# One first transfer for weight half, tokens and gains; latent attention twelve steps later in a two-layer trunk on one core

## The chip, the core and the metric

The kernel runs on one core of a Trainium2 chip. The metric is the device time of one execution in microseconds (us). The runs of the kernel before took 802.56, 802.88 and 804.34 us, with a median of 802.88 us. The execution that was profiled took 802.21 us; its span, from the first instruction to the last, is 800.4 us.

## The reference

Two layers run over 256 tokens of 1024 numbers, in fp32. The part that matters here:

```python
for l in range(DEPTH):
    h = rmsnorm(x, g_pre_mix[l])
    (c_q, c_kv, k_r, p_in, s_u, s_v, cv_b, cv_c, cv_x,
     gate_logits) = split_cols(h @ w_in[l])
    y_a = mla_branch(c_q, c_kv, k_r, ...) @ w_br_a[l]     # latent attention
    y_b = pool_branch(p_in, ...) @ w_br_b[l]
    y_c = sgu_branch(s_u, s_v, ...) @ w_br_c[l]
    y_d = conv_branch(cv_b, cv_c, cv_x, ...) @ w_br_d[l]
    gates = sigmoid(gate_logits).reshape(B, S, N_BRANCH, D)
    merged = sum over the four branches of gate * y
    x = x + rmsnorm(merged @ w_out[l], g_post_mix[l])
    h = rmsnorm(x, g_pre_ffn[l])
    f = (silu(h @ w_ffn_gate[l]) * (h @ w_ffn_up[l])) @ w_ffn_down[l]
    x = x + rmsnorm(f, g_post_ffn[l])
```

In `mla_branch` the normed `c_q` goes through `w_uq`, the normed `c_kv` through `w_ukv`, and eight heads of a chunk-causal softmax follow.

## The kernel before

**Precision by halves.** Every product is made of three matmuls (`mac`, L318 to L320). A number a is held as a high half (a rounded to TensorE's fast fp32 format, by ScalarE) and a low half (a minus its high half, by VectorE); the kernel adds high times high, low times high and high times low. So each weight that arrives must be split twice, the high half on ScalarE (L268) and then the low half on VectorE (L288), before its last use.

**Pieces.** The weights are cut on the host into pieces of at most 128 x 1024 floats, in the order of use, which `piece_plan` writes out. A piece is fetched by SyncE (SP) into one of four staging buffers `st` (`stage`, L253), split into two of 24 buffers `u`, and used. SP waits at a fetch until the staging buffer's former piece has been split. "A" are the 416 columns of the projection that feed the attention (query latent, key-value latent, rotary key), "S" the 512 of the gating unit, "P" and "C" 512 each for the pooling, the convolution and the rest; each has four pieces, of two 128-row blocks k each. "gd", "gb", "gc" and "ga" are the gates' pieces of the branches in the order d, b, c, a; "y" are the branch projections; "uq" (two) and "ukv" are the attention's own weights.

**Steps.** The kernel has no scheduler: instructions stand on each engine in the order in which the program writes them. The matmuls are written unit by unit, a unit being two blocks of one piece for one half h of the tokens (six matmuls of 512 columns), and after each unit `tick` is called, which is one step. A step also advances the background generators, among them `g_att` (latent attention) and `g_misc` (the three other branches), whose `yield n` says how many steps to let pass, and it splits another piece while fewer than five or six untouched ones are ready (`LOW`, `HIGH`). `AS` is the number of steps after which the attention starts, counted from its spawn at step 16 of layer 0, and `PA` the steps between the scaling of its latents and their transposes. In layer 0 the attention starts at step 23, its first projection (uq) runs at step 35, its last product of probabilities and values (L743) at step 81, and the first unit that needs it, the branch projection of a, comes at step 108. Layer 1 has the same distances.

**The start.** Until the first weights are there, TensorE multiplies a tile of zeros `NW` = 7 times (L387). The first inputs come on two queues. ScalarE's queue fetches block 0 of the transposed tokens (`xT`) and then the table `const` (158 columns: rotary tables, pooling counts and, from column 96, the gains). SP's queue fetches, each as a transfer of its own, the first halves of pieces A0 and S0, block 1 of the tokens, the second halves, blocks 2 and 3, the whole pieces A1 and S1, and blocks 4 to 7. The tokens are scaled by the gain while they are split (`x_hi`: block 0 on VectorE, L561, the others on ScalarE, L563; `x_lo` on VectorE, L567), and the halves of A0 and S0 are split at L581 and L582. TensorE's first real matmuls are the 24 of L909, twelve for block 0 (six of 416 columns, six of 512) and twelve for block 1; then the units of A1, S1, A2 and so on follow.

Of the kernel before, what the change touches and what calls it, by code (L numbers as in the profile page):

```python
# [10 lines left out]
F32 = mybir.dt.float32  # L11
F32R = mybir.dt.float32r
# [5 lines left out]
P = 128  # L18
# [18 lines left out]
NTOK = 9  # L37
LOW = 4
GF = 5
GY, MY, AY, AS, MS = 4, 4, 4, 8, 3  # L40
Y1, Y2, Y3, Y4, Y5 = 2, 4, 3, 3, 3
PA, PB = 2, 4
SA, SB = 3, 3
NW = 7
EV = 2
XAT, XD = (8, 9), 8
RN = 1
# [23 lines left out]
SGW = _o  # L71


def down_after(b):

    return [b - DLAG] if 0 <= b - DLAG < NB - DLAST else []


def piece_plan():

    plan = []
    for l in range(NL):
# [111 lines left out]


@with_exitstack
def trunk(ctx: ExitStack, tc, x, xT, wall, small, const, qtab, gpost, out):
    nc = tc.nc
    PS = bass.MemoryType.PSUM
    cp = ctx.enter_context(tc.tile_pool(name="cp", bufs=1))  # L200
# [156 lines left out]


    ident = T([P, P], "ident", 1, pool=cp)
    cst = T([P, 96 + NL * SGW], "cst", 1, pool=cp)  # L360
    warm = T([P, 1], "warm", 1, pool=cp)
    ht = [hT_tiles(h) for h in range(2)]
    state["free"] -= 2
# [6 lines left out]
    nc.scalar.dma_start(cst, const)  # L370
# [12 lines left out]
    nc.vector.memset(warm, 0.0)  # L383
# [170 lines left out]
    sg = gains(0)  # L554
    hT, rstd = [None, None], [None, None]

    def x_hi(k, eng=nc.scalar):
        for h in range(2):
            o, i, g = ht[h][0][:, k, :], xt[k // 4][:, k % 4, h * P:(h + 1) * P], sg["gpm"][:, k:k + 1]
            if eng is nc.vector:  # L560
                nc.vector.tensor_scalar(o, i, g, None, op0=ALU.mult)  # L561
            else:
                nc.scalar.activation(o, i, AF.Identity, scale=g)  # L563

    def x_lo(k):
        for h in range(2):
            nc.vector.scalar_tensor_tensor(ht[h][1][:, k, :], xt[k // 4][:, k % 4, h * P:(h + 1) * P],  # L567
                                           sg["gpm"][:, k:k + 1], ht[h][0][:, k, :].bitcast(F32),
                                           op0=ALU.mult, op1=ALU.subtract)


    first_w = {i: (U([P, PIECE], F32R), U([P, PIECE], F32R)) for i in range(2)}
    state["free"] -= 4
    src = [staged.pop(i) for i in range(2)]
    for k in range(2):
        x_hi(k, nc.vector if k == 0 else nc.scalar)
        x_lo(k)
        for i in range(2):
            w = PLAN[i][1] // 2
            c = np.s_[:, k * w:k * w + w]  # L580
            nc.scalar.activation(first_w[i][0][c], src[i][c], AF.Copy)  # L581
            nc.vector.tensor_tensor(first_w[i][1][c], src[i][c], first_w[i][0].bitcast(F32)[c], op=ALU.subtract)  # L582
    for i in range(2):
        known(i, *first_w[i])
    state["cv"] = 2
# [608 lines left out]
def build(arrays):  # L1194
# [3 lines left out]
    ap = {k: nc.dram_tensor(k, v.shape, F32, kind="ExternalInput").ap() for k, v in arrays.items()}  # L1198
    out = nc.dram_tensor("out", (SEQ, D), F32, kind="ExternalOutput").ap()
    with tile.TileContext(nc) as tc:  # L1200
        trunk(tc, ap["x"], ap["xT"], ap["wall"], ap["small"], ap["const"], ap["qtab"], ap["gpost"], out)
    return nc


def host_arrays(inputs):
    inp = {k: np.asarray(v) for k, v in inputs.items()}
    wall = np.zeros((len(PLAN), P, PIECE), np.float32)
    for i, (key, w) in enumerate(PLAN):
        wall[i, :, :w] = host_piece(inp, key)
    x = np.ascontiguousarray(inp["x"][0])  # L1210
    const, qtab = host_const(inp)
    return {
        "x": x,
        "xT": np.ascontiguousarray(x.T.reshape(NK, P, SEQ).transpose(1, 0, 2)),
        "wall": wall,
        "small": np.stack([host_small(inp, l) for l in range(NL)]),
        "const": const,
        "qtab": qtab,
        "gpost": np.ascontiguousarray(np.stack([inp["g_post_mix"], inp["g_post_ffn"]], axis=1)),
    }  # L1220
# [9 lines left out]
```

## Time and profile before

| what | value |
|---|---|
| median of 3 runs | 802.88 us |
| profiled execution | 802.21 us |
| its span | 800.4 us |
| TensorE busy | 790.8 us (99%) |
| VectorE busy | 598.3 us (75%) |
| ScalarE busy | 452.6 us (57%) |
| moved by DMA | 148.11 MB, mean 185 GB/s |
| from the span's start to the first matmul of L909 | 5.67 us |

A row of the timeline gives the start and the length in us, the engine (PE is TensorE, PEld its weight load, DVE VectorE, ACT ScalarE, a q behind it the engine's queue of instructions), the line, the operation, the tiles written and read, the shape, the count, and in brackets how long the engine had been idle and what ended that. In the DMA view a row gives the tile and its source, the queue, the count, the size and the time from the issue to the landing.

### The profile page before, as it was taken

To read this page: it belongs to the slowest core of one execution; us is meant where nothing else is said; L and a number is where in the kernel's file an instruction comes from. 1 tells how busy PE (TensorE), PEld (TensorE's weight loads), DVE (VectorE), ACT (ScalarE), POOL (GpSimd) and SP (SyncE) were. 2 spreads that over 40 slices of the span, in tenths; PEclk is the share of its full clock that TensorE was granted. 3 is DMA by queue.
4 is the path that set the end of the run, shared out by engine and by line. 5 is a ranking of instruction groups with operands and counts; after the bars stand their busy time and mean duration, and the time that the engine had idled before them with its cause. 6 is when DMAs were issued, how large, how long until landed. Compare 5 with 4: busy or idle time off the path is not lost.

```text
span 800.4 us, 10903 instructions
## 1 busy us (share of the span) xinstructions
PE 790.8 (99%) x3982; PEld 666.3 (83%) x3982; DVE 598.3 (75%) x1094; ACT 452.6 (57%) x776; POOL 3.9 (0%) x16
## 2 busy tenths in 40 slices
PE   8999999999999999999999999999999999999996
PEld 8888887888888888888888888878888888888885
DVE  6687976758887777778895688764679787777773
ACT  7767655444665555455665675644367555455541
POOL 0000000000000000000000000000000000000000
PEclk9999999999999999999999999999999999999999
DMA  9866444465664565555655545455555555555631
GB/s 317 304 215 212 160 158 158 160 208 164 201 214 136 185 205 185 186 192 176 223 170 197 205 161 182 131 172 197 175 193 184 181 185 186 187 185 185 206 106 52
DMA packets 42245, 148.11 MB, mean 185 GB/s; under 512 B 4688, under 2 KB 5840, under 8 KB 42192
## 3 DMA queue, kind: packets, MB, share of 16 engines
q1 hardware_dynamic: 41328, 145.12, 54.4%
q0 software_dynamic: 576, 2.10, 0.8%
q8 instruction: 31, 0.51, 0.3%
q10 hardware_dynamic: 288, 0.21, 0.1%
q14 instruction: 22, 0.18, 0.1%
HBM read 146.36 MB, written 1.05 MB: 184 GB/s over the span
## 4 chain that ended last, share of the span: by engine, by line
PE 98%; DVE 1%; DMA 0%; ACT 0%; issue 0%; DVEq 0%; SPq 0%; ACTq 0%
PE acc L318 20%; PE acc L320 20%; PE acc L319 20%; PE mm L1097 17%; PE mm L1102 9%; PE tp L440 3%; PE mm L318 2%; PE mm L320 2%; PE mm L319 2%; PE mm L715 1%; PE acc L743 1%; PE acc L909 1%; DMA st<-wall 0%; PE mm L836 0%; PE mm L862 0%; DVE mrg L500 0%
## 5 line engine op out<-in xcount | busy, mean ns | idle before, releaser
L288 DVE TENSOR_TENSOR u<-st,u 128x1024 fp32r<-128x1024 f32 (+1 forms) x268 | 318.6, 1214 | 50.6 <-ACT u L268 50.0
L268 ACT ACTIVATE u<-st 128x1024 fp32r<-128x1024 f32 (+1 forms) x268 | 273.5, 1047 | 17.0 <-DMA st<-wall 16.8
L318 PE MATMUL acc<-u,hh 128*128 128x512 f32 (+1 forms) x424 | 169.1, 399 | 0.0
L320 PE MATMUL acc<-u,hh 128*128 128x512 f32 (+1 forms) x424 | 164.5, 388 | 0.0
L319 PE MATMUL acc<-u,hl 128*128 128x512 f32 (+1 forms) x424 | 164.2, 387 | 0.0
L1097 PE MATMUL mm<-u,u 128*128 128x512 f32 x576 | 144.4, 392 | 0.0
L1097 PEld LDWEIGHTS mm<-u,u 128*128 128x128 f32 x576 | 105.3, 188 | 20.8
L318 PE MATMUL acc<-u,s2k 128*128 128x512 f32 x256 | 101.2, 395 | 0.0
L320 PE MATMUL acc<-u,s2k 128*128 128x512 f32 x256 | 100.6, 393 | 0.0
L319 PE MATMUL acc<-u,s2k 128*128 128x512 f32 x256 | 100.3, 392 | 0.0
L320 PEld LDWEIGHTS acc<-u,hh 128*128 128x128 f32 x424 | 79.6, 188 | 16.2
L318 PEld LDWEIGHTS acc<-u,hh 128*128 128x128 f32 x424 | 79.7, 188 | 14.5 <-issue 0.3
L319 PEld LDWEIGHTS acc<-u,hl 128*128 128x128 f32 x424 | 79.8, 188 | 14.2
L1102 PEld LDWEIGHTS mm<-u,u 128*128 128x128 f32 x576 | 78.6, 190 | 5.6
L1102 PE MATMUL mm<-u,u 128*128 128x256 f32 x576 | 80.3, 282 | 0.0
L1025 ACT ACTIVATE gate<-acc,rhalf 128x512 f32<-128x512 f32 x32 | 22.0, 689 | 65.9 <-PE acc L320 65.7
L320 PEld LDWEIGHTS acc<-u,s2k 128*128 128x128 f32 x256 | 48.1, 188 | 10.1
L318 PEld LDWEIGHTS acc<-u,s2k 128*128 128x128 f32 x256 | 48.2, 188 | 9.3 <-issue 0.3
L319 PEld LDWEIGHTS acc<-u,s2k 128*128 128x128 f32 x256 | 48.1, 188 | 9.1
L1108 DVE TENSOR_TENSOR tok<-mm,tok 128x256 f32<-128x256 f32 x72 | 30.3, 420 | 27.7 <-ACT tok L1107 27.5
L1107 ACT COPY tok<-mm 128x256 f32<-128x256 f32 x72 | 26.6, 370 | 42.6 <-PE mm L1102 39.6
L443 ACT ACTIVATE s2k<-tok 128x256 fp32r<-128x256 f32 (+1 forms) x38 | 16.3, 429 | 53.8 <-DVE tok L1122 53.8
(172 smaller groups left out, 750.1 us busy)
## 6 DMA issues: line engine op xcount, KB each, us to landing
st<-wall SPq DMA_DIRECT2D x261, 512.0 KB, 3.8
st<-wall SPq DMA_DIRECT2D x7, 416.0 KB, 4.0
gpost<-gpost POOLq DMA_DIRECT2D x4, 512.0 KB, 4.7
x<-x SPq DMA_DIRECT2D x2, 512.0 KB, 6.0
small<-small SPq DMA_DIRECT2D x2, 512.0 KB, 4.2
u<-xT SPq DMA_DIRECT2D x3, 256.0 KB, 6.2
st<-wall SPq DMA_DIRECT2D x2, 256.0 KB, 4.3
out<-x SPq DMA_DIRECT2D x2, 256.0 KB, 2.0
```

The lines of the kernel that those rows point to most:

```text
L268: nc.scalar.activation(hi[:, :w], st[:, :w], AF.Copy)
L288: nc.vector.tensor_tensor(lo[:, :w], st[:, :w], hi.bitcast(F32)[:, :w], op=ALU.subtract)
L318: nc.tensor.matmul(out_, a[0][aw], w[0][ws], start=start, stop=False)
L319: nc.tensor.matmul(out_, a[1][aw], w[0][ws], start=False, stop=False)
L320: nc.tensor.matmul(out_, a[0][aw], w[1][ws], start=False, stop=stop)
L440: nc.tensor.transpose(dst[:, i * P:(i + 1) * P], s, ident)
L443: nc.scalar.activation(hi, src, AF.Copy)
L1025: nc.scalar.activation(gt[h], pgt[h], AF.Tanh, scale=rhalf[h])
L1097: nc.tensor.matmul(o, pc_[0][:, k * P:(k + 1) * P], hx[k // 2][:, k % 2].rearrange("p s t -> p (s t)"), start=(k == 0), stop=False)
L1102: nc.tensor.matmul(o[:, :SEQ], pc_[1][:, k * P:(k + 1) * P], hx[k // 2][:, k % 2, 0, :], start=False, stop=(k == NK - 1))
L1107: nc.scalar.copy(dst, o[:, SEQ:2 * SEQ])
L1108: nc.vector.tensor_tensor(dst, o[:, 0:SEQ], dst, op=ALU.add)
```

## The change

1. A new input `head` holds, side by side, the first half of A0, block 0 of the tokens and eight columns of gains (680 columns); and in a second part the second half of A0, block 1 of the tokens and the whole table (830 columns). Each part is one transfer on SP's queue into a staging buffer, from which the tokens, the weights and the gains are read directly. ScalarE's queue fetches nothing any more. The table is copied to its own tile `cst` by ScalarE, after the second parts of A0 and S0 have been split.
2. Piece A1 is fetched and split in halves too, between the tokens' blocks 2 and 3. S1, blocks 4 and 5, A2, and blocks 6 and 7 are fetched later in SP's order, behind the copy of the table in the program; S1 has to wait for the staging buffer of the first part.
3. The zeros are multiplied eight times (`NW`).
4. `AS` goes from 8 to 20 and `PA` from 2 to 5: the attention starts at step 35, uq at step 50, the last product of probabilities and values stands at step 96. Its three weight pieces move in the plan behind the eight gate pieces of branch d.

The diff, cut to its core:

```diff
-GY, MY, AY, AS, MS = 4, 4, 4, 8, 3
+GY, MY, AY, AS, MS = 4, 4, 4, 20, 3
-PA, PB = 2, 4
+PA, PB = 5, 4
-NW = 7
+NW = 8
+HA = 416
+HC = HA + SEQ
+HG = SG["gpm"][1]
+CW = 96 + NL * SGW
...
-        plan += [((l, "uq", i), 1024) for i in range(2)]
-        plan += [((l, "ukv", 0), 1024)]
...
+                if br == "b" and n == 0:
+                    plan += [((l, "uq", i), 1024) for i in range(2)]
+                    plan += [((l, "ukv", 0), 1024)]
...
-    xt_load(nc.scalar, 0, 1)
-    nc.scalar.dma_start(cst, const)
-    stage_part(0, 0)
+    heads = [T([P, PIECE], "st", NST, pool=wp)]
+    nc.sync.dma_start(heads[0][:, 0:HC + HG], head[0, :, 0:HC + HG])
     stage_part(1, 0)
-    xt_load(nc.sync, 1, 2)
-    stage_part(0, 1)
+    heads.append(T([P, PIECE], "st", NST, pool=wp))
+    nc.sync.dma_start(heads[1][:, 0:HC + CW], head[1, :, 0:HC + CW])
     stage_part(1, 1)
-    state["dma"] = 2
     xt_load(nc.sync, 2, 4)
-    stage_to(4)
-    xt_load(nc.sync, 4, 6)
-    xt_load(nc.sync, 6, 8)
+    stage_part(2, 0)
+    stage_part(2, 1)
+    state["dma"] = 3
...
+    nc.scalar.copy(cst, heads[1][:, HC:HC + CW])
+    stage_to(4)
+    xt_load(nc.sync, 4, 6)
+    for k in range(2):
+        x_hi(2 + k)
+        x_lo(2 + k)
+        split_part(2, k, src[2][:, HA * k:HA * k + HA])
...
     stage_to(5)
-    for kp in range(1, 4):
+    xt_load(nc.sync, 6, 8)
+    pump(1)
+    settle()
+    for kp in range(2, 4):
```

ScalarE's instructions from the program's start: `u` are split weights, `hh` split tokens, `st` staging buffers, `warm` a dummy. Before:

```order
L367 DMA u_8_76<-xT 128x256
L370 DMA cst_70<-const 128x158
L388 ACT_TABLE_LOAD
L388 ACTIVATE warm_71<-warm_71 128x1
L581 ACTIVATE u_18_112<-st_80 128x416
L581 ACTIVATE u_20_114<-st_82 128x512
L563 ACTIVATE hh_4_72<-u_8_76,cst_70 128x128
L563 ACTIVATE hh_6_74<-u_8_76,cst_70 128x128
L581 ACTIVATE u_18_112<-st_80 128x416
L581 ACTIVATE u_20_114<-st_82 128x512
```

And after, to the same place and on to the first half of A1, which stands between the tokens' blocks:

```order
L394 ACT_TABLE_LOAD
L394 ACTIVATE warm_71<-warm_71 128x1
L590 ACTIVATE u_19_109<-st_78 128x416
L590 ACTIVATE u_21_111<-st_80 128x512
L579 ACTIVATE hh_4_72<-st_82 128x128
L579 ACTIVATE hh_6_74<-st_82 128x128
L590 ACTIVATE u_19_109<-st_82 128x416
L590 ACTIVATE u_21_111<-st_80 128x512
L602 COPY cst_70<-st_82 128x158
L579 ACTIVATE hh_4_72<-u_8_76,cst_70 128x128
L579 ACTIVATE hh_6_74<-u_8_76,cst_70 128x128
L590 ACTIVATE u_23_113<-st_86 128x416
```

The two DMAs are gone from ScalarE, block 1 of the tokens is read from the second head transfer (`st_82`), and the copy of the table has come in ahead of block 2.

SP's queue at the same place, before and after:

```order
L261 DMA st_80<-wall 128x416
L261 DMA st_82<-wall 128x512
L367 DMA u_8_76<-xT 128x256
L261 DMA st_80<-wall 128x416
L261 DMA st_82<-wall 128x512
L367 DMA u_8_76<-xT 128x512
L253 DMA st_88<-wall 128x832
L253 DMA st_90<-wall 128x1024
L367 DMA u_9_77<-xT 128x512 x2
```

```order
L377 DMA st_78<-head 128x680
L268 DMA st_80<-wall 128x512
L380 DMA st_82<-head 128x830
L268 DMA st_80<-wall 128x512
L374 DMA u_8_76<-xT 128x512
L268 DMA st_86<-wall 128x416 x2
L260 DMA st_132<-wall 128x1024
L374 DMA u_9_77<-xT 128x512
L260 DMA st_147<-wall 128x832
```

S1 (`st_132`) is the fourth piece and takes the buffer of the first head transfer; blocks 4 and 5 of the tokens stay right behind it, and A2 now stands ahead of blocks 6 and 7.

TensorE around the last product of probabilities and values of layer 0, before (step 81, among the units of the second gate group of branch c) and after (step 96, among those of the first group of branch a):

```order
L318 MATMUL acc_1470<-u_295_1335,hh_4_72 128x512
L319 MATMUL acc_1470<-u_295_1335,hl_5_73 128x512
L320 MATMUL acc_1470<-u_296_1336,hh_4_72 128x512
L743 MATMUL acc_1168<-tok_1453,u_180_833 64x128 x4
L318 MATMUL acc_1471<-u_285_1295,hh_6_74 128x512
```

```order
L325 MATMUL acc_1552<-u_315_1432,hh_6_74 128x512
L326 MATMUL acc_1552<-u_315_1432,hl_7_75 128x512
L327 MATMUL acc_1552<-u_316_1433,hh_6_74 128x512
L772 MATMUL acc_1332<-tok_1612,u_224_1035 64x128 x4
L325 MATMUL acc_1552<-u_324_1477,hh_6_74 128x512
```

The same four matmuls stand fifteen units later. But for the eighth product of zeros, TensorE has the same instructions in both kernels.

More of the change, by code (lines that the diff above doesn't have):

```diff
@@ L196, in trunk @@
 @with_exitstack
-def trunk(ctx: ExitStack, tc, x, xT, wall, small, const, qtab, gpost, out):
+def trunk(ctx: ExitStack, tc, x, xT, wall, small, head, qtab, gpost, out):
     nc = tc.nc
@@ L359, in trunk @@
     ident = T([P, P], "ident", 1, pool=cp)
-    cst = T([P, 96 + NL * SGW], "cst", 1, pool=cp)
+    cst = T([P, CW], "cst", 1, pool=cp)
     warm = T([P, 1], "warm", 1, pool=cp)
@@ L367, in xt_load @@
         eng.dma_start(xt[k0 // 4][:, k0 % 4:k0 % 4 + k1 - k0, :], xT[:, k0:k1, :])
-    xt_load(nc.scalar, 0, 1)
-    nc.scalar.dma_start(cst, const)
-    stage_part(0, 0)
+    heads = [T([P, PIECE], "st", NST, pool=wp)]
+    nc.sync.dma_start(heads[0][:, 0:HC + HG], head[0, :, 0:HC + HG])
     stage_part(1, 0)
-    xt_load(nc.sync, 1, 2)
-    stage_part(0, 1)
+    heads.append(T([P, PIECE], "st", NST, pool=wp))
+    nc.sync.dma_start(heads[1][:, 0:HC + CW], head[1, :, 0:HC + CW])
     stage_part(1, 1)
-    state["dma"] = 2
     xt_load(nc.sync, 2, 4)
-    stage_to(4)
-    xt_load(nc.sync, 4, 6)
-    xt_load(nc.sync, 6, 8)
+    stage_part(2, 0)
+    stage_part(2, 1)
+    state["dma"] = 3
+    wt = tok()
     wt = tok()
@@ L555, in trunk, with x_in, x_gain @@
     hT, rstd = [None, None], [None, None]
+    def x_in(k, h):
+        if k < 2:
+            return heads[k][:, HA + h * P:HA + h * P + P]
+        return xt[k // 4][:, k % 4, h * P:(h + 1) * P]
+    def x_gain(k):
+        if k == 0:
+            return heads[0][:, HC:HC + 1]
+        return heads[1][:, HC + 97:HC + 98] if k == 1 else sg["gpm"][:, k:k + 1]
     def x_hi(k, eng=nc.scalar):
         for h in range(2):
-            o, i, g = ht[h][0][:, k, :], xt[k // 4][:, k % 4, h * P:(h + 1) * P], sg["gpm"][:, k:k + 1]
+            o, i, g = ht[h][0][:, k, :], x_in(k, h), x_gain(k)
             if eng is nc.vector:
@@ L566, in x_lo, with split_part @@
         for h in range(2):
[L567 to L574, printed above, removed]
+            nc.vector.scalar_tensor_tensor(ht[h][1][:, k, :], x_in(k, h), x_gain(k),
+                                           ht[h][0][:, k, :].bitcast(F32), op0=ALU.mult, op1=ALU.subtract)
+    def split_part(i, k, src):
+        w = PLAN[i][1] // 2
+        c = np.s_[:, k * w:k * w + w]
+        nc.scalar.activation(first_w[i][0][c], src, AF.Copy)
+        nc.vector.tensor_tensor(first_w[i][1][c], src, first_w[i][0].bitcast(F32)[c], op=ALU.subtract)
+    first_w = {i: (U([P, PIECE], F32R), U([P, PIECE], F32R)) for i in range(3)}
+    state["free"] -= 6
+    src = [None, staged.pop(1), staged.pop(2)]
     for k in range(2):
@@ L577, in trunk @@
         x_lo(k)
[L578 to L583, printed above, removed]
+        split_part(0, k, heads[k][:, 0:HA])
+        split_part(1, k, src[1][:, 512 * k:512 * k + 512])
+    nc.scalar.copy(cst, heads[1][:, HC:HC + CW])
[5 more added lines that the diff above has]
+        split_part(2, k, src[2][:, HA * k:HA * k + HA])
+    for i in range(3):
         known(i, *first_w[i])
-    state["cv"] = 2
+    state["cv"] = 3
     stage_to(5)
-    for kp in range(1, 4):
+    xt_load(nc.sync, 6, 8)
+    pump(1)
+    settle()
+    for kp in range(2, 4):
         for k in range(2 * kp, 2 * kp + 2):
@@ L1200, in build @@
     with tile.TileContext(nc) as tc:
-        trunk(tc, ap["x"], ap["xT"], ap["wall"], ap["small"], ap["const"], ap["qtab"], ap["gpost"], out)
+        trunk(tc, ap["x"], ap["xT"], ap["wall"], ap["small"], ap["head"], ap["qtab"], ap["gpost"], out)
     return nc
@@ L1211, in host_arrays @@
     const, qtab = host_const(inp)
+    xT = np.ascontiguousarray(x.T.reshape(NK, P, SEQ).transpose(1, 0, 2))
+    head = np.zeros((2, P, HC + CW), np.float32)
+    for k in range(2):
+        head[k, :, 0:HA] = wall[0, :, k * HA:(k + 1) * HA]
+        head[k, :, HA:HC] = xT[:, k, :]
+    head[0, :, HC:HC + HG] = const[:, 96:96 + HG]
+    head[1, :, HC:] = const
     return {
         "x": x,
-        "xT": np.ascontiguousarray(x.T.reshape(NK, P, SEQ).transpose(1, 0, 2)),
+        "xT": xT,
         "wall": wall,
         "small": np.stack([host_small(inp, l) for l in range(NL)]),
-        "const": const,
+        "head": head,
         "qtab": qtab,
```

## The prediction, made before the changed kernel ran

> **What bounds the kernel now.** I read the page first. Its first part and its chain say that TensorE is nearly all of the span:
>
> ```profile
> PE 790.8 (99%) x3982; PEld 666.3 (83%) x3982; DVE 598.3 (75%) x1094; ACT 452.6 (57%) x776; POOL 3.9 (0%) x16
> PE 98%; DVE 1%; DMA 0%; ACT 0%; issue 0%; DVEq 0%; SPq 0%; ACTq 0%
> ```
>
> So only what TensorE loses can be won. The table of waits for its matmuls has two rows in the whole span, and the same table for its weight loads after 12.4 us has this as its first:
>
> ```profile
> PE acc L909 <- ACT u L581: 1.3, 1, 1.3
> PE mm L387 <- DVE warm L383: 1.1, 1, 1.1
> ```
>
> ```profile
> PEld acc L743 <- issue: 3.9, 11, 0.4
> ```
>
> Behind the start nothing is waited for longer than 0.4 us, and those idle loads lie beside running matmuls (the matmuls' own table has no row there). The loss is at the start, which the timeline shows; its last six rows are the first matmuls of A1 (12.43), of S1 (14.70) and of A2 (17.47):
>
> ```profile
> 0.74 0.85 SPq L261 DMA_DIRECT2D st<-wall  x2
> 1.05 3.36 PE L387 MATMUL mm<-tok 128*128 128x128 f32 x14 [1.05 <-DVE warm L383]
> 1.18 0.45 ACTq L370 DMA_DIRECT2D cst<-const  x1
> 2.11 0.91 SPq L261 DMA_DIRECT2D st<-wall  x2
> 3.50 0.55 ACT L581 ACTIVATE u<-st 128x416 fp32r<-128x416 f32 x1 [0.34 <-DMA st<-wall]
> 4.95 0.63 ACT L581 ACTIVATE u<-st 128x512 fp32r<-128x512 f32 x1 [0.90 <-DMA st<-wall]
> 5.24 0.48 DVE L561 TENSOR_SCALAR hh<-u,cst 128x128 fp32r<-128x128 f32 x2 [4.23 <-DMA cst<-const]
> 5.63 0.61 DVE L567 SCALAR_TENSOR_TENSOR hl<-u,cst,hh 128x128 fp32r<-128x128 f32 x2
> 5.67 1.03 PE L909 MATMUL acc<-u,hh 128*128 128x416 f32 x2 [1.26 <-ACT u L581]
> 5.77 0.69 ACT L563 ACTIVATE hh<-u,cst 128x128 fp32r<-128x128 f32 x2 [0.20 <-DMA u<-xT]
> 6.16 1.19 DVE L582 TENSOR_TENSOR u<-st,u 128x416 fp32r<-128x416 f32 x2
> 7.20 1.75 PE L909 MATMUL acc<-u,hh 128*128 128x416 f32 x4
> 10.65 1.02 PE L909 MATMUL acc<-u,hh 128*128 128x416 f32 x4
> 10.74 1.06 ACT L268 ACTIVATE u<-st 128x1024 fp32r<-128x1024 f32 x1 [0.30 <-DMA st<-wall]
> 11.84 1.22 DVE L288 TENSOR_TENSOR u<-st,u 128x1024 fp32r<-128x1024 f32 x1 [0.33 <-ACT u L268]
> 12.43 0.35 PE L318 MATMUL acc<-u,hh 128*128 128x416 f32 x1
> 12.62 0.35 PE L319 MATMUL acc<-u,hl 128*128 128x416 f32 x1
> 14.70 0.40 PE L318 MATMUL acc<-u,hh 128*128 128x512 f32 x1
> 14.94 0.40 PE L319 MATMUL acc<-u,hl 128*128 128x512 f32 x1
> 15.17 0.40 PE L320 MATMUL acc<-u,hh 128*128 128x512 f32 x1
> 17.47 0.35 PE L318 MATMUL acc<-u,hh 128*128 128x416 f32 x1
> ```
>
> Two losses are to be seen. TensorE stands idle from 4.41 (1.05 + 3.36) to 5.67, 1.26 us. The row names ScalarE, but VectorE's L561 is the later cover: it waited 4.23 us for the table. And the first matmuls run slowly: the same four (two low-half ones of 416 columns, two of 512) take 1.75 us at 7.20 and 1.02 us at 10.65. Steady steps are 0.19 (12.43 to 12.62) and 0.23 us (14.94 to 15.17), so twelve matmuls of one block should take 6 x 0.19 + 6 x 0.23 = 2.5 us and the 24 of L909 5.0; they took 12.43 - 5.67 = 6.76. The slow rate cost 1.75 us. Its end shows in the windows, cut where the matmuls' spacing changes:
>
> ```profile
> 5.67:9.24 3.57, 3.57 (x10) 3.18 (x11) 3.57 (x11) 2.74 (x7) 0.00 (x0) 1.00 1.00 365
> 9.24:12.43 3.19, 3.19 (x16) 2.78 (x15) 2.42 (x6) 2.89 (x7) 0.00 (x0) 1.00 1.04 401
> ```
>
> Ten matmuls are busy in 3.57 us, then sixteen in 3.19. (The column of the granted clock, 1.00 in both, is no help: the trace holds no record of the clock before 9.24.) I read this as a clock at half rate that opened at 9.24, 3.57 us after the real matmuls began; the zeros, busy for 3.36 us and followed by the hole, did not open it.
>
> **The first transfer.** The DMA view, asked for short stretches of issue, gives what landed when:
>
> ```profile
> st<-wall SPq DMA_DIRECT2D x1, 208.0 KB, 2.7
> u<-xT ACTq DMA_DIRECT2D x1, 128.0 KB, 2.9
> ```
>
> ```profile
> st<-wall SPq DMA_DIRECT2D x1, 208.0 KB, 4.6
> cst<-const ACTq DMA_DIRECT2D x1, 79.0 KB, 3.9
> ```
>
> The table landed at 1.18 + 3.9 = 5.1, and that disappears: eight columns of it now come with the first transfer. That one has 128 x 680 x 4 bytes = 340 KB. Before, 208 KB on one queue and 128 KB on the other, 336 KB together, had landed by 0.74 + 2.9 = 3.6, so I take 3.55 for 340 KB on one queue; the ends are 3.44 (the 208 KB alone) and 4.9 (the next 256 KB, split at 4.95). ScalarE's 416 columns take 0.55: 4.1. VectorE's 0.48 for both token halves lies beside it. About 0.1 us of signalling (5.58 to 5.67 in the rows) makes 4.2. The zeros now end later: a pass takes about (3.36 - 0.42)/13 = 0.22, two more bring the next matmul to 4.65. That is the later of the two, so the real matmuls start at 4.65, **1.02 us earlier** and without a hole. The eighth product costs nothing as long as the data is later than 4.2; if the data were there at 4.1 it costs 0.4 at most. Giving up ScalarE's queue puts nothing on SP ahead of the first issue (0.74 either way).
>
> The Trainium skill says on its page "DMA: Bandwidth & Descriptors", section "Issuing engines are not separate DMA queues", that transfers from all engines run on the same 16 DMA engines and a second queue saves only issue time. The rows agree as far as they go (two queues delivered 336 KB by 3.6); by the rule one queue costs nothing, as assumed.
>
> **What is late next.** Block 1 now hangs on the second head transfer, 415 KB, with 340 + 256 + 415 = 1011 KB queued up to its end. Before, 1007 KB (208 + 256 + 128 + 208 on SP, 207 on ACT) were queued up to the second half of A0, which landed at 2.11 + 4.6 = 6.7. Fewer small rows and two transfers fewer should help: the earliest is 5.6, by the rates of the DMA view in slices of 0.4 us:
>
> ```profile
> GB/s 0 0 0 0 79 285 366 365 292 261 298 349 302 260 230 290 366 358 380 378 444 400 428 379 410 401 419 392 430 370 400 400 345 392 372 192 191 365 287 287
> ```
>
> The nine slices up to 5.2 moved 1.04 MB, as much as is queued here, and some 0.4 us pass to the landing. I take 6.3, nearer to the row with the same queue. Behind it stand, on ScalarE in order, block 1's two token halves (0.69) and the 416 columns (0.55), so 7.6 with 0.1 of signalling. Twelve matmuls of block 0 end at 4.65 + 2.5 = 7.15 at full rate, and later by half of each slow microsecond. So up to about 0.9 us at the slow rate is free, and **block 1 starts at 7.6**. Ends for this: 7.15 (TensorE's own) and 8.0.
>
> From 7.6, block 1 takes 2.5: 10.1. The table's copy on ScalarE (128 x 158, between 0.35, half of the row of two token halves, and the 0.55 of 416 columns) delays blocks 2 and 3 and the halves of A1; I reckon A1's second low half ready 0.2 late. A1 and S1 then take 2.3 + 2.75 = 5.0: A2 would begin at 15.3 instead of 17.47. S1's cover: it now waits for the buffer of the first transfer, free when VectorE has split its weights at about 5.3 (3.55 + 0.05 + 0.48 + 0.61 + 0.6, the last half of the row at 6.16). Before, S1 was split from 10.74 on because of what was queued ahead. That queue is the same length, so S1 lands at 10.3 to 10.7 if it joins the queue before that runs dry; its high half is ready at 11.8 and the low half at 13.0, needed at 12.6 + 0.46. That is the thinnest cover; if it goes, a few tenths. A2 and all later pieces are ready 2 us or more before TensorE wants them: the pooling pieces, the slowest, show it, with the second one's low half ready at 24.62 + 1.22 = 25.84 and its first matmul at 28.78:
>
> ```profile
> 24.62 1.22 DVE L288 TENSOR_TENSOR u<-st,u 128x1024 fp32r<-128x1024 f32 x1 [0.38 <-ACT u L268]
> ```
>
> ```profile
> 28.78 0.39 PE L318 MATMUL mm<-u,hh 128*128 128x512 f32 x1
> ```
>
> So the start is worth 17.47 - 15.3 = **2.15 us**, and behind it the trace shows no wait to swallow it.
>
> **The attention.** No matmul is added or removed but for the zeros. In layer 0 the last product of probabilities and values ends at 143.3, and the merged branches, four units behind the first use, are transposed at 185.8:
>
> ```profile
> 142.61 0.66 PE L743 MATMUL acc<-tok,u 128*64 128x128 f32 x8
> ```
>
> ```profile
> 185.77 0.49 PE L440 MATMUL tp<-ident,mrg 128*128 128x128 f32 x3
> ```
>
> Between steps 81 and 112 that is 1.4 us a step; fifteen steps later is 164, still 16 us ahead of need. VectorE was busy 14.33 of 20 us in the stretch where the heaviest attention work lay:
>
> ```profile
> 100.00:120.00 20.00, 20.00 (x100) 16.41 (x99) 14.33 (x30) 10.49 (x21) 0.00 (x0) 1.00 0.48 158
> ```
>
> It has room. Different neighbours at the transposes could change TensorE by some tenths either way; I take 0 and allow 0.4.
>
> **The sum.** 802.21 - 2.15 = 800.1 for an execution like the profiled one, whose span and 1.8 us around it are one run. The median stands 0.67 higher; I add half, as the moment at which the clock opens is probably what differs: 800.4.
>
> **The rivals.** 0.2% of the median is 1.6 us, about what a measurement of this kernel can tell from no change.
> (1) The clock opens late, again 3.57 us after the real matmuls began, at 8.2, as if the zeros counted for nothing. For it: they opened nothing before. Against: now no hole follows them. Block 0 then takes six slow steps of 0.35 and about three and a half of 0.43 to 8.2, ends at 8.8, and A2 starts at 8.8 + 7.5 = 16.3: gain 1.2, 801.0 to 801.7 by the median.
> (2) The second head transfer lands at 5.6 and the clock opens during the zeros: TensorE's own 7.15 counts, and the gain is 2.8 (1.02 + 1.75): 799.7.
> (3) The first transfer isn't earlier: on one queue its 340 KB need until 4.9, as the next 256 KB did. The matmuls start at 5.55, with a hole behind the zeros and the slow rate as before; the gain is 0.1 and the time 802.4.
> (4) Slower: with uq and ukv behind branch d's pieces, all three are first used in steps 50 to 54, so the stock of untouched pieces falls from five to three while VectorE also clears the projection and computes the pooling. If a splitting falls behind there, TensorE waits for branch b's gate pieces: one ACT and one DVE splitting, 1.06 + 1.22 = 2.3 us, in each of two layers. It decides from the point where VectorE's work in a step exceeds the step; it had 5.7 of 20 us free in its fullest stretch, which speaks against it. 800.4 + 4.6 = 805.0.
>
> The Trainium skill's page "TensorE: Matmul & The Clock Gate" (Part 1) holds that the clock opens after a window of about 3.4 us, free-running, in which TensorE is busy. The trace agrees: 3.36 us opened nothing, 3.57 did. By it the clock would open anywhere from 4.5 to 7.9, which lies between my sum and rival 1.
>
> **How the numbers follow.** Forecast 0.50, of its own 799.9 to 801.1; rival 1 0.22, half of it within 0.2%; rival 2 0.13; rival 3 0.09; rival 4 0.06. Faster: 0.50 + 0.11 + 0.13 = 0.74; same 0.11 + 0.09 = 0.20; slower 0.06. The range, 799.2 to 802.2, takes in rival 2 with its 0.4, rival 1 and half of 3.
>
> **What would show it.** L909 starting near 4.65 without an idle time behind L387; the four-matmul row of block 0 shorter than 1.75; ScalarE waiting for the second head transfer until about 6.3; A2 near 15.3; no new row in TensorE's waits. I am wrong if the zeros are followed by a hole, if the slow rate lasts past 8, or if a wait appears at steps 50 to 57 or at branch a.

## The result, and the profile after

The changed kernel takes 811.53 us (median of six runs, 809.57 to 812.61); the kernel before took 802.72 us (six runs, 802.15 to 804.34). The ratio is 1.0104, with a 95% interval of 1.0086 to 1.0122. The change costs 8.8 us; the forecast was 800.4 us. Executions that were disturbed as a whole, such as one of 2,815 us met below, are left out of all comparisons.

The execution that was profiled took 809.70 us, its span is 807.9 us. Its page, the lines that answer to the first two of before:

```profile
PE 795.0 (98%) x3984; PEld 664.8 (82%) x3984; DVE 598.8 (74%) x1095; ACT 451.0 (56%) x778; POOL 3.9 (0%) x16
PE 93%; DVE 4%; ACT 2%; DMA 1%; issue 0%; SPq 0%; DVEq 0%; ACTq 0%
```

TensorE is busy for 4.2 us more, with only two matmuls more, and the span is 7.5 us longer; the chain that ended last now goes through VectorE for 4% of the span. The table of waits of TensorE's matmuls (total, times, longest) has a new first row:

```profile
PE mm L865 <- DVE tok L860: 4.5, 4, 1.5
PE mm L393 <- DVE warm L389: 1.1, 1, 1.1
PE acc L938 <- ACT u L590: 0.6, 1, 0.6
```

L865 is the product of the pooling branch (before L836), two products of two matmuls each in each layer (so four waits in all), and L860 the last line of the chain of VectorE operations that computes the pooled tokens. The timeline of layer 0 shows the place:

```profile
61.83 0.69 DVE L837 TENSOR_TENSOR tok<-tok,tok 128x512 f32<-128x512 f32 x1
62.44 1.22 DVE L295 TENSOR_TENSOR u<-st,u 128x1024 fp32r<-128x1024 f32 x1
63.96 0.17 DVE L425 SCALAR_TENSOR_TENSOR ry<-ra,ry 128x4 f32<-128x4 f32 x1
64.16 2.46 DVE L694 COPY u<-tp 64x1024 f32<-64x1024 f32 x2
68.90 0.72 DVE L844 TENSOR_TENSOR tok<-tok 128x542 f32<-128x542 f32 x1
71.22 1.22 DVE L295 TENSOR_TENSOR u<-st,u 128x1024 fp32r<-128x1024 f32 x1
71.87 0.40 PE L327 MATMUL acc<-u,hh 128*128 128x512 f32 x1
73.81 0.70 PE L865 MATMUL mm<-tok,small 128*128 128x256 f32 x2 [1.54 <-DVE tok L860]
75.24 0.70 PE L865 MATMUL mm<-tok,small 128*128 128x256 f32 x2 [0.73 <-DVE tok L860]
```

Between the convolution's last operation (61.83) and the pooling chain (68.90) VectorE now ends the attention's reciprocal root (L425) and makes the two copies of the rotated key (L694). In the kernel before, those copies ran at 47.00, ahead of the convolution, and the pooling product had no wait (67.54 is the convolution's first operation on VectorE there):

```profile
47.00 2.46 DVE L665 COPY u<-tp 64x1024 f32<-64x1024 f32 x2
67.54 0.47 DVE L806 SCALAR_TENSOR_TENSOR tok<-tok,cst,tok 128x256 f32<-128x256 f32 x1
```

```profile
83.57 1.17 PE L836 MATMUL mm<-tok,small 128*128 128x256 f32 x4
```

TensorE also comes to that product sooner: at 72.27 (71.87 + 0.40) instead of 83.57. The product stands behind the same unit as before (step 47), but the attention's own products, which filled the time from step 35 on, now begin at step 50, behind it.

The start, in the changed kernel's timeline (the last row is the first matmul of A2):

```profile
1.05 3.79 PE L393 MATMUL mm<-tok 128*128 128x128 f32 x16 [1.05 <-DVE warm L389]
3.54 0.55 ACT L590 ACTIVATE u<-st 128x416 fp32r<-128x416 f32 x1 [1.31 <-DMA st<-head]
4.49 1.04 PE L938 MATMUL acc<-u,hh 128*128 128x416 f32 x2
5.76 1.00 PE L938 MATMUL acc<-u,hh 128*128 128x416 f32 x4
7.13 0.69 ACT L579 ACTIVATE hh<-st 128x128 fp32r<-128x128 f32 x2 [1.68 <-DMA st<-head]
8.31 0.65 PE L938 MATMUL acc<-u,hh 128*128 128x416 f32 x2 [0.64 <-ACT u L590]
16.07 0.35 PE L325 MATMUL acc<-u,hh 128*128 128x416 f32 x1
```

The real matmuls start at 4.49 with no hole behind the zeros, TensorE's granted clock opened to the full rate at 5.44 (9.24 before), block 1 waits until 8.31 for the second head transfer, and A2 begins at 16.07 instead of 17.47: 1.40 us are won.

A third thing appears when the 3,360 matmuls of the units and the feed-forward part are lined up in order in the two traces ("lined up" means this below, too). Outside the attention, where the two programs are alike, the changed kernel still loses 0.9 us in 213 (2.24 us behind at 167.91 of before, 3.15 behind at 380.80). The steps of the 512-column matmuls whose stationary operand is a tile `s2k` are longer. First and last of 17 such matmuls in a row, 16 steps, in the kernel before and then in the changed one:

```profile
380.11 0.39 PE L319 MATMUL acc<-u,s2k 128*128 128x512 f32 x1
383.78 0.39 PE L320 MATMUL acc<-u,s2k 128*128 128x512 f32 x1
```

```profile
383.25 0.40 PE L326 MATMUL acc<-u,s2k 128*128 128x512 f32 x1
386.98 0.40 PE L327 MATMUL acc<-u,s2k 128*128 128x512 f32 x1
```

That is 3.67 us against 3.73. Over all 749 such steps that no wait disturbs, the means are 229.1 and 233.5 ns. The pool that holds `s2k` places its tiles in the order in which they are first named. The attention names `s2k` first before, and comes behind the merge buffers and the gates after; so the ten `s2k` tiles moved from bytes 182,496 to 202,975 of each partition to bytes 207,200 to 227,679.

So there were three candidates: the start (-1.4), two waits for VectorE, and an address.

### The profile page after: what moved, and what is told of

The parts are those of the page before. It is cut to its first block, busy times and chain, and to the rows that moved or that the text cites. A ratio compares the mean times of both kernels' runs of the same rounds, so it can differ in the third digit from the quotient of the medians.

```text
span 807.9 us, 10923 instructions
## 1 busy us (share of the span) xinstructions
PE 795.0 (98%) x3984; PEld 664.8 (82%) x3984; DVE 598.8 (74%) x1095; ACT 451.0 (56%) x778; POOL 3.9 (0%) x16
## 3 DMA queue, kind: packets, MB, share of 16 engines
HBM read 146.36 MB, written 1.05 MB: 182 GB/s over the span
## 4 chain that ended last, share of the span: by engine, by line
PE 93%; DVE 4%; ACT 2%; DMA 1%; issue 0%; SPq 0%; DVEq 0%; ACTq 0%
PE acc L325 19%; PE acc L327 19%; PE acc L326 19%; PE mm L1126 16%; PE mm L1131 8%; PE tp L446 3%; PE mm L325 2%; PE mm L327 2%; PE mm L326 2%; PE mm L744 1%; PE acc L772 1%; DVE u L295 1%; DMA st<-head 1%; ACT u L275 0%; DVE tok L857 0%
## 5 line engine op out<-in xcount | busy, mean ns | idle before, releaser
L325 PE MATMUL acc<-u,s2k 128*128 128x512 f32 x256 | 103.3, 404 | 0.0
L326 PE MATMUL acc<-u,s2k 128*128 128x512 f32 x256 | 101.2, 395 | 0.0
L327 PE MATMUL acc<-u,s2k 128*128 128x512 f32 x256 | 101.2, 395 | 0.0
L449 ACT ACTIVATE s2k<-tok 128x256 fp32r<-128x256 f32 (+1 forms) x38 | 16.3, 428 | 53.9 <-DVE tok L1151 53.9
```

The source lines that it names most:

```text
L325: nc.tensor.matmul(out_, a[0][aw], w[0][ws], start=start, stop=False)
L326: nc.tensor.matmul(out_, a[1][aw], w[0][ws], start=False, stop=False)
L327: nc.tensor.matmul(out_, a[0][aw], w[1][ws], start=False, stop=stop)
L449: nc.scalar.activation(hi, src, AF.Copy)
```

## The experiments

All comparisons are with runs of the kernel before on the same chip (802.57 to 802.89 us by the median).

**The two halves of the change.** The start alone is the changed kernel with the numbers and the plan of the attention put back:

```diff
-GY, MY, AY, AS, MS = 4, 4, 4, 20, 3
+GY, MY, AY, AS, MS = 4, 4, 4, 8, 3
-PA, PB = 5, 4
+PA, PB = 2, 4
+        plan += [((l, "uq", i), 1024) for i in range(2)]
+        plan += [((l, "ukv", 0), 1024)]
         plan += [((l, "C", i), wd["C"]) for i in range(4)]
```

> The changed kernel with the attention put back to its old twelve steps and its three pieces back to the old place; only the new start is left. My theory (the start gains 1.4 us by A2's first matmul, nothing behind it loses): 802.7 - 1.4 = 801.3, A2 begins at 16.1, no row for the pooling product in TensorE's waits, 512-column steps with the state tiles s2k as stationary operand at 229 ns. Rival (the start itself upsets something behind it, for instance the ring of pieces runs two units longer): over 802.7, with a new wait in the table.

Measured: 802.78 us, ratio 1.0001 (0.9992 to 1.0010). The expected 1.4 us were not there. The same kernel was run again:

> The new start alone once more: its first profile fell on an execution that took 2,815 us, and its timed runs gave 802.8 where 801.3 was expected, so the trace of an ordinary execution has to show where the 1.4 us went. Theory A (the start wins 1.3 to 1.4 us by A2's first matmul and something behind it gives them back): A2 begins at 16.1, and a later place of the trace, shown by lining up its matmuls with those of the kernel before, loses 1.3 us. Theory B (with the old plan the start itself wins nothing): A2 begins at 17.3 or later.

Measured: 802.61 us, ratio 0.9991 (0.9981 to 1.0000). Theory A: lined up, it is 1.33 us ahead at 37.39 us of before, 0.06 ahead at 42, and 0.62 us behind at 50.05. The first loss, 1.27 us, is two waits of TensorE at the pieces of C (timeline of the start alone, TensorE and ScalarE):

```profile
32.84 1.06 ACT L274 ACTIVATE u<-st 128x1024 fp32r<-128x1024 f32 x1 [1.09 <-DMA st<-wall]
35.53 1.06 ACT L274 ACTIVATE u<-st 128x1024 fp32r<-128x1024 f32 x1 [1.13 <-DMA st<-wall]
37.90 0.50 PE L326 MATMUL acc<-u,hh 128*128 128x512 f32 x1 [0.32 <-DVE u L294]
39.92 0.50 PE L326 MATMUL acc<-u,hh 128*128 128x512 f32 x1 [0.36 <-DVE u L294]
```

ScalarE waits over 1 us for each of these weight transfers: up to about 40 us the stream of pieces is the limit, not TensorE. In the kernel before it waits there too (1.93, 1.05 and 0.56 us), but TensorE still has some cover. The rows of the same two pieces in the kernel before, and a window, which ends with the DMA's busy share and GB/s:

```profile
34.74 1.06 ACT L268 ACTIVATE u<-st 128x1024 fp32r<-128x1024 f32 x1 [0.56 <-DMA st<-wall]
35.84 1.23 DVE L288 TENSOR_TENSOR u<-st,u 128x1024 fp32r<-128x1024 f32 x1 [0.89 <-ACT u L268]
37.86 1.23 DVE L288 TENSOR_TENSOR u<-st,u 128x1024 fp32r<-128x1024 f32 x1 [0.80 <-ACT u L268]
28.00:36.00 8.00, 8.00 (x37) 6.63 (x36) 5.36 (x9) 4.46 (x6) 0.00 (x0) 1.00 0.87 289
```

There the low halves are ready at 37.07 and 39.09, and the two matmuls that waited above start at 38.75 and 40.11: a cover of 1.7 and 1.0 us. With the new start TensorE comes 1.33 us sooner, and the pieces come 0.8 us later (the split at 34.74 now stands at 35.53), which is more than the cover. The three pieces uq and ukv stand in the stream ahead of C here. No run moved these three alone; the changed kernel, which fetches C ahead of them, still has 1.25 of its 1.40 us at 42 us. The second loss, 0.7 us at the transposes of the attention's latents from 46 to 50 us, is not shown to come from the start: two kernels below that keep the old start and the old attention lose 0.3 and 0.6 us at the same place.

The attention alone is the other half of the diff, in the kernel before.

> The kernel before with the attention twelve steps later and its three pieces behind branch d's; the old start stays. My theory (5.4 us from two waits of 2.7 us for the pooling chain, and 3.3 us from 768 slower matmul steps): 802.7 + 8.7 = 811.4, with TensorE's waits showing the pooling product behind VectorE's pooling chain, about 2.7 us in each layer, and A2 at 17.5 as before. Rival (the loss needs both parts, since the earlier start brings the pieces and the VectorE work together): 803 to 807.

Measured: 813.08 us, ratio 1.0129 (1.0114 to 1.0145). The pooling product waits as in the changed kernel, in the same table:

```profile
PE mm L837 <- DVE tok L832: 4.5, 4, 1.5
```

The loss needs nothing of the new start. Two of its runs took 811.6 and 811.8 us, as expected; the other two, at 814.4 and 814.6, had a mean clock of 0.993 instead of 0.997, of which more below.

**The addresses.** Two unused tiles, named ahead of the others, put the tiles back to their old addresses in the changed kernel, with every instruction in its place:

```diff
+        if l == 0:
+            T([P, 4, 32], "kr", 2)
+            T([P, 2, SEQ], "s2k", 10, F32R)
         sm = small_load(l)
```

> The changed kernel in its own order, but with the tiles of the small pool at the addresses that they have in the kernel before (two unused tiles are named earlier, so that the pool lays its tiles out in the old order). Theory A (the place of the s2k tiles in the buffer sets the matmul's step): 512-column steps with s2k as stationary operand fall from 233.5 back to 229 ns, the time falls by 3.3 us to about 806.3 in its best runs, and the wait for the pooling chain stays at 2.7 us in each layer. Theory B (the step is slower because other VectorE and ScalarE work now runs beside these matmuls): steps stay at 233.5 ns and the time at 809.6 or more.

Measured: 807.65 us, 806.23 in its best run, ratio 1.0059 (1.0046 to 1.0071). The step is back at 229.2 ns, and the 16 steps quoted take 3.67 us again (381.86 to 385.53).

The opposite edit names the tiles in the kernel before so that they get the new addresses.

> The kernel before in its own order, but with the tiles of the small pool at the addresses of the changed kernel (unused tiles are named earlier). Theory A (the place of the s2k tiles sets the matmul's step): their 512-column steps go from 229.1 to 233.5 ns, and with some 770 of them the time rises by 3.3 us to 806.0. Theory B (it is the neighbouring work): 802.7, steps of 229 ns.

Measured: 806.42 us, ratio 1.0046 (1.0031 to 1.0061), 3.6 us more, with the step at 233.5 ns:

```profile
382.22 0.39 PE L320 MATMUL acc<-u,s2k 128*128 128x512 f32 x1
385.95 0.39 PE L318 MATMUL acc<-u,s2k 128*128 128x512 f32 x1
```

Not one instruction stands elsewhere in this kernel, so the addresses alone cost it: 749 steps of 4.4 ns are 3.3 us. A third place, below the old one:

> The kernel before with the s2k tiles 23,488 bytes lower in the buffer of each partition (from 182,496 to 159,008), the tiles that stood there moved up behind them. Theory A (the step of a 512-column matmul grows with the address of its stationary operand: 226.8 ns at 36,000 to 114,000, 228 at 143,000 to 155,000, 229.1 at 182,000 to 201,000, 233.5 at 207,000 to 226,000): 228.3 ns, so 0.6 us less, 802.1. Theory B (only the region above 203,000 is slow): no change, 802.7.

Measured: 802.06 us, ratio 0.9992 (0.9983 to 1.0001): 228.3 ns, as theory A had it, but the time isn't resolved from no change. Theory A's rule, a step that grows with the address, does not hold for all matmuls: its 226.8 ns at the low addresses are the 92 steps of one branch projection (`acc<-u,u`), and the 584 steps of 512 columns in the feed-forward part, whose stationary operands lie as low (below 126,240), have a mean of 229.9 ns in the kernel before. What is shown is the dependence for the `s2k` tiles.

**The wait.** First, the pooling product three steps later in TensorE's order:

```diff
-            yield 3
+            yield 6
             pm = mm()
```

> The changed kernel with the pooling product three steps later in TensorE's order and nothing else. Theory A (the stall is a plain wait for the pooling chain, with slack behind it): both waits go, 5.4 us less, about 804.2, and the slow steps of 233.5 ns stay. Theory B (VectorE is simply behind by then, and the next thing that TensorE needs from it, the split gate pieces, is late by as much): a wait of 1 to 2.7 us in each layer turns up at another product, and the time stays within 2 us of 809.6.

Measured: 813.96 us, ratio 1.0137 (1.0122 to 1.0153). Theory B, and worse than it. TensorE's waits:

```profile
PE acc L327 <- DVE u L295: 5.5, 2, 2.8
```

The product waits no more; the next thing that TensorE needs from VectorE, the low half of a gate piece, is late by as much. So it is not one product that stands too early. VectorE's queue is behind as a whole.

Second, the key copies on ScalarE, to take 2.46 us from that queue (the old addresses as well):

```diff
-                nc.vector.tensor_copy(kT[e][rows], t[rows, 0:SEQ].unsqueeze(1).to_broadcast([64, 4, SEQ]))
+                nc.scalar.copy(kT[e][rows], t[rows, 0:SEQ].unsqueeze(1).to_broadcast([64, 4, SEQ]))
```

> The changed kernel with the old addresses (as in the run with the old layout, 806.2 at best) and the two copies of the rotated key, 2.46 us of VectorE ahead of the pooling chain, given to ScalarE. Theory A (VectorE's own queue is what makes the pooling product late): the wait for the pooling chain shrinks from 2.7 us to 0.3 or less in each layer, the clock stays open, and the time is 806.2 - 4.8 = 801.4. Theory B (ScalarE is as full there, so the split pieces that VectorE waits for come later by as much): the wait stays above 1.5 us in each layer and the time at 804 or more.

Measured: 814.52 us, ratio 1.0138 (1.0121 to 1.0155): theory B, and worse. The wait grew:

```profile
PE mm L865 <- DVE tok L860: 8.6, 4, 3.6
```

The timelines of ScalarE and VectorE say why:

```profile
64.27 0.51 ACT L687 ACTIVATE u<-u,ry 128x256 f32<-128x256 f32 x1 [3.04 <-DVE ry L425]
65.78 2.03 ACT L694 COPY u<-tp 64x1024 f32<-64x1024 f32 x2
67.71 1.06 ACT L275 ACTIVATE u<-st 128x1024 fp32r<-128x1024 f32 x1
68.66 0.62 ACT L449 ACTIVATE s2k<-tok 128x512 fp32r<-128x512 f32 x1
69.31 0.69 DVE L450 TENSOR_TENSOR s2k<-tok,s2k 128x512 fp32r<-128x512 f32 x1 [5.08 <-ACT s2k L449]
```

ScalarE stands 3.04 us for VectorE's reciprocal root (as it does in the changed kernel); then the copies (2.03) stand in front of ScalarE's half of the split of the convolution's result (L449). VectorE, which had 0.54 us of wait there in the changed kernel, now waits 5.08 us for it, with the pooling chain behind. The two queues hold each other up in turn, and a step taken from one is paid in the other.

Third, only the front of the projection (sums of squares, rotated key, root, key copies) back to its old steps, all else of the attention as changed:

```diff
-GY, MY, AY, AS, MS = 4, 4, 4, 20, 3
+GY, MY, AY, AS, MS = 4, 4, 4, 8, 3
-PA, PB = 5, 4
+PA, PB = 17, 4
```

> The changed kernel with the old addresses, and of the attention only the front of the projection (sums of squares, rotated key, their transposes and the two key copies) put back to its old steps 23 to 28; the rest of the projection, the scores and the three pieces stay where the change put them. Theory A (the collision in steps 34 to 50 is between that front and the pooling chain, and the new plan keeps the gain of the start): no wait for the pooling chain, the clock stays open, and the time is 802.7 - 1.3 = 801.4. Theory B (the front at its old place costs what it cost with the start alone, since ScalarE is full from 36 to 44 us): no wait for the pooling chain, but 1.9 us lost between 38 and 50 us, 803.3. Theory C (another part of the later attention makes the pooling product late): the wait stays, 806.

Measured: 801.12 us, ratio 0.9979 (0.9970 to 0.9988). Theory A. TensorE's table of waits has one row left, the one before the zeros:

```profile
PE mm L393 <- DVE warm L389: 1.1, 1, 1.1
```

In the stretch from 57 to 75 us (span, then busy time of TensorE, of its loads, of VectorE, ScalarE, POOL), first the changed kernel and then this one:

```profile
57.00:75.00 18.00, 15.97 (x75) 12.55 (x73) 15.71 (x33) 9.54 (x18) 0.38 (x3) 1.00 0.43 150
```

```profile
57.00:75.00 18.00, 17.86 (x84) 14.47 (x83) 13.94 (x30) 9.92 (x17) 1.15 (x4) 1.00 0.64 229
```

VectorE has 13.94 us of work there instead of 15.71, and TensorE loses 0.14 instead of 2.03. Lined up with the run with the old addresses, from which it differs only in the place of that front, this kernel is 2.4 us ahead behind the pooling product of layer 0 and 6.8 ahead at the end. And it is still 1.40 us ahead of the kernel before at 42 us, where the start alone had lost its gain; uq and ukv no longer stand ahead of C here. Half of that is spent by the end of layer 0's attention: lined up, it is 0.64 us ahead at 167.91 and 0.76 at the last matmul.

The spans differ by more, 1.3 us, and the rest is an accident. From the last matmul to the end the kernel before takes 7.69 us, and the four traced kernels with the old start take 7.67 to 7.69; the nine with the new start take 7.04 to 7.10. At its end the program reads eight completion counters one after another, and its transfers take these counters in turn. In the kernel before the last transfer falls on the counter that is read first, and the seven other readings follow it, some 0.06 us each; the new start has two transfers fewer, so the last one falls on the seventh (on the eighth in the last kernel below, which has one more), and the readings ahead of it are done while it is under way.

> The same, but with the s2k tiles at 159,008 instead of 182,496, where the kernel before was 0.7 us faster. By theory A 801.4 - 0.7 = 800.7; by theory B 802.6; a candidate for a version that beats both kernels.

Measured: 800.23 us, ratio 0.9971 (0.9960 to 0.9981), a version that beats both kernels; it is 0.9 us below its twin on the same chip by the median, with steps of 228.6 instead of 229.2 ns. The 749 steps account for 0.4 us of that; the runs of either kernel spread over more than the rest. The cover at the pooling product is thin: here TensorE waits 0.5 us for the chain in layer 0.

The front half way:

> As the run with the early front, but with the front in steps 29 to 34 (half way between the kernel before and the changed one). Theory A (a collision with the pooling chain alone, which begins at step 34 with transposes on TensorE and at step 38 or so on VectorE): the wait is gone or below 0.5 us in each layer, 801.4 to 802.4. Theory C (the chain is late for another reason): the wait stays at 2.7 us, 806.

Measured: 807.81 us, ratio 1.0061 (1.0049 to 1.0073). Neither theory: there is no wait for the pooling chain, but another one, of the same size.

```profile
PE tp L446 <- DVE u L694: 5.6, 2, 3.0
```

The front takes one of the two transpose buffers when it begins and frees it with the key copies; now the other branches' transposes, which come at step 34, want it in between. So the front has two places to avoid, and its old steps avoid both.

**The second head transfer.** The last kernel takes the table out of it:

```diff
-    nc.sync.dma_start(heads[1][:, 0:HC + CW], head[1, :, 0:HC + CW])
+    nc.sync.dma_start(heads[1][:, 0:HC], head[1, :, 0:HC])
     stage_part(1, 1)
+    nc.sync.dma_start(cst, head[1, :, HC:HC + CW])
```

> The kernel with the early front and the low s2k tiles (800.2), with the table taken out of the second head transfer: that one has 672 columns (344 KB) instead of 830 (425 KB), its gain comes from the eight columns in the first transfer, and the table follows by itself behind the second half of S0. Theory A (block 1 waits for the bytes queued up to the end of the second head transfer, which move at about 0.3 MB a us): it lands 0.2 to 0.3 us earlier, block 1 starts at 7.7 to 7.9 instead of 7.9 to 8.3, and the time falls by 0.2 us, which is below what these runs can tell. Theory B (the landing is set by the spread of the packets over the queues, 0.4 us from one execution to the next, not by 81 KB): landing between 6.4 and 6.8 as in the three executions before, and nothing changes.

(The transfers are of 336 and 415 KB; the text on record has them a little too large.) Measured: 800.83 us, ratio 0.9978 (0.9969 to 0.9987). Theory A in direction: the DMA view gives 4.7 us from the issue to the landing, where the eight traced executions with the table in the transfer had 5.1 to 5.7. The size, at least 0.4 us, is more than its 0.2 to 0.3, and this is one execution.

```profile
st<-head SPq DMA_DIRECT2D x1, 336.0 KB, 4.7
```

Block 1 starts at 7.62 without a wait. But two new waits follow, at S1, whose transfer now stands one place further back:

```profile
13.09 0.50 PE L325 MATMUL acc<-u,hh 128*128 128x512 f32 x1 [0.48 <-ACT u L275]
14.35 0.50 PE L327 MATMUL acc<-u,hh 128*128 128x512 f32 x1 [0.53 <-DVE u L295]
```

The 0.55 us won at block 1 over the kernel with the table in the transfer is more than lost by A2, which begins at 16.76 instead of 15.93. At the pooling product of layer 0 the two are level again, as the other one waits there and this one, coming later, doesn't; at the last matmul this one is 0.16 us ahead, and the times show nothing of it.

**The clock.** The times of the changed kernel come in three groups, and the mean granted clock of each run goes with them: 809.57 and 809.70 us at 0.997 and 0.998, 810.81 at 0.995, 812.25 to 812.61 at 0.993. The trace of the run with the old addresses holds the cause. By its records the granted clock opens (to the full rate) at 4.568, closes (to half) at 472.194 and opens again at 475.608: 467.626 us are 137 times 3.413, the closed time is once that. Windows of 3.41 us on that grid, where the wait of layer 1 falls:

```profile
468.78:472.19 3.41, 1.19 (x5) 0.55 (x4) 3.18 (x14) 0.00 (x0) 0.00 (x0) 1.00 0.49 154
472.19:475.61 3.42, 3.42 (x9) 2.66 (x9) 2.17 (x5) 2.28 (x5) 0.00 (x0) 0.50 0.00 0
```

The clock was at half rate in the window that followed one in which TensorE was busy for 1.19 us. In the changed kernel's trace the grid lay elsewhere (it opened at 5.436), and the same waits left more work in each window; the clock stayed open:

```profile
70.30:73.71 3.41, 1.97 (x11) 1.27 (x8) 3.26 (x10) 0.00 (x0) 0.00 (x0) 1.00 0.44 154
469.66:473.07 3.41, 1.79 (x7) 0.86 (x5) 3.25 (x12) 0.00 (x0) 0.00 (x0) 1.00 0.49 175
```

With the product three steps later it closed in both layers:

```profile
76.67:80.08 3.41, 0.97 (x4) 0.84 (x5) 2.42 (x5) 2.02 (x5) 0.00 (x0) 1.00 0.00 0
80.08:83.49 3.41, 3.41 (x15) 3.23 (x15) 2.97 (x6) 1.89 (x3) 0.00 (x0) 0.50 0.49 161
```

All traces agree. There are six closings in them, each right behind a window of the grid in which TensorE was busy for 0.65 to 1.19 us; the least busy window that no closing followed had 1.72. In two cases (the key copies on ScalarE, the front half way) the window behind the closing wasn't filled either, and the clock stayed at half rate for 6.827 us. And it opened, at the start of the thirteen traces compared here, at the end of the first window of the grid that TensorE filled: in the kernel before, the window from 2.41 to 5.82 held 2.15 us of work, and the next was full and ended at 9.24.

One closing of one window costs 1.5 us: lined up with the kernel with the early front, the run with the old addresses falls from 5.26 to 6.78 us behind in the slow window. For the runs without a trace of their own this is an inference from their mean clock, not shown.

## Why the prediction was wrong

**The start** was right in its mechanism. The first transfer landed at 3.5 (0.74 + 2.8; 3.55 was taken), the real matmuls came at 4.49 (4.65 was taken), without a hole, the clock opened early (5.44 instead of 9.24), and block 1 was late next. The mis-sized term is the landing of the second head transfer: 6.3 was taken; in the changed kernel's trace ScalarE was released by it at 7.13, and in the eight traces that have this transfer between 6.75 and 7.42. With the same working behind it (0.69 + 0.55 + 0.1), that makes 8.5 instead of 7.6 for block 1 (measured 8.31), and the gain at A2 was 1.40 instead of 2.15. S1 was called the thinnest cover; it held in the change, and gave way in the kernel in which block 1 came earlier and the transfer of S1 one place later.

**"Behind it the trace shows no wait to swallow it"** failed. The start alone is worth nothing (802.78 and 802.61). No wait of TensorE stood there in the trace of before, because pieces that arrive just in time leave none. The step that failed is "A2 and all later pieces are ready 2 us or more before TensorE wants them": it was read off the pooling pieces, and the pieces of C, further on, had 1.7 and 1.0 us, of which the new start itself took 0.8 by fetching later. What should have been read is ScalarE, waiting for each weight transfer, and the DMA share of 0.87 to 0.89 from 28 to 44 us. The move of uq and ukv, which the prediction costed at nothing, goes with a gain that holds past C: with it and the early front, the time is 801.12.

**"The attention: 0, allow 0.4"** failed, and this is the step that turned the sign. The reason given was a stretch, 100 to 120 us, in which VectorE had 5.7 of 20 us free. That stretch is where the attention was heaviest, not where its moved part would meet other work. The front of the projection landed on the steps of the convolution and the pooling, and in the 18 us from 57 to 75 VectorE had 15.71 us of work, in an order in which ScalarE and VectorE waited for each other. TensorE, without the attention's matmuls ahead of it, came to the pooling product 11 us sooner, and the chain was not done. That cost 2.4 us in layer 0 and 2.9 in layer 1, and up to twice 1.5 for the clock.

**Rival 4**, with a chance of 0.06, had the engine, both layers and nearly the price (4.6; measured 5.3), but not the place or the waiter, so that the price agrees is in part luck. It looked at steps 50 to 57, where uq and ukv are first used and the stock of ready pieces falls (the program's marks for that stock are `LOW` = 4 and `HIGH` = 6, not five and six). The wait came at step 47, ahead of these, for the pooling chain; the gate pieces were waited for only once that product was moved three steps back. "It had 5.7 of 20 us free in its fullest stretch, which speaks against it" is the same false reason.

**The address** was in no term and no rival: 3.3 to 3.6 us from tiles that moved 24,704 bytes up without an instruction being touched.

The sum, at the last matmul of the profiled executions: the kernel with the early front is 0.8 us ahead of before, the waits cost 2.4 + 2.9, the addresses 3.5, together 8.0; lined up, the changed kernel is 8.1 us behind (7.5 by the spans, for the 0.6 us of the counters at the end, which was in no term either). The median of the changed kernel, 811.53, is higher than this execution by a closing of the clock; that step is inferred.

The Trainium skill's page "TensorE: Matmul & The Clock Gate" (Part 1) has the clock gate work in free-running windows of about 3.4 us, and close after an idle one. The length and the free running agree with the records here (137 x 3.413). That a window must be idle does not: 1.19 busy us of 3.41 closed it, 1.72 did not. The prediction took 3.36 busy us of zeros as too few to open the clock, and the hole behind them as the reason; by the records, what counts is how much of one window of the grid is filled, and in the kernel before the window from 2.41 to 5.82, with the hole in it, held only 2.15 us of work.

## What to carry to other kernels

When a block of work is moved, look at the busy time and at the order of the helping engines in the stretch where it will land, side by side with what already runs there; a mean, or the fullest stretch of before, says nothing about it. A gain ahead of a stream that is itself the limit is lost again unless something is taken out of the stream there, so ask which engine waits for the transfers behind the gain. And compare the addresses of the stationary operands before and after: naming a tile earlier or later can move hundreds of matmul steps by 2%.

## What the runs showed of the hardware

- The step of a 512-column fp32r matmul with an `s2k` tile as its stationary operand depended on where these tiles lie in the partition: 228.3 and 228.6 ns at bytes 159,008 to 179,487 (two kernels), 229.1 and 229.2 at 182,496 to 202,975, 233.5 at 207,200 to 227,679. Between the kernel before and the one with the new addresses no instruction differs in place. Address alone does not set the step of every matmul (229.9 ns in the feed-forward part, below 126,240). Why is open.
- The clock closed behind windows of 3.413 us that were busy for 0.65 to 1.19 us (six cases), and never behind one of 1.72 or more. Whether a wait of some 2 us falls into one window is a matter of the grid's place in the run. This gives two or three groups of times for one kernel (the part of the groups is inferred).
- The clock opened at the end of the first window that TensorE filled: between 4.57 and 6.02 us in the nine traces of the new start, where zeros run into the real matmuls without a hole, and between 9.24 and 10.12 in the four with the hole.
- Eight completion counters are read one after another at the end, some 0.06 us each. Which of them the last transfer falls on was worth 0.6 us: 7.67 to 7.69 us behind the last matmul in four traces, 7.04 to 7.10 in nine.
